# First projections interleaved by k-tile, and matmul operands re-placed within 64 bytes

## The chip, the cores and the metric

The kernel runs on one core of a Trainium2 chip. The metric is device time in microseconds (us). Before the change two timed runs gave 1695.17 and 1696.14 us, median 1695.66. One further execution was profiled, with a span of 1693.5 us from its first to its last instruction. All durations below are from that one execution.

## What is computed

Two transformer blocks are applied to 256 tokens of width 2048, in fp32. What matters here is that nearly all arithmetic is a product of the 256 tokens with a large weight matrix.

```python
def first_block(x, ...):
    h = rmsnorm(x, pre_mix_g)
    q_a, k_a, v_a, q_b, k_b, v_b, f_b = split(h @ w_in)
    o_a = swa_sink_attention(q_a, k_a, v_a, sinks)          # 16 heads of 64
    o_b = forgetting_attention(q_b, k_b, v_b, log_sigmoid(f_b + b_forget))
    x = x + rmsnorm(concat(rmsnorm(o_a), rmsnorm(o_b)) @ w_out, post_mix_g)
    gate, val = split(causal_dwconv(rmsnorm(x, pre_ffn_g) @ w_up, conv_w, conv_b))   # 2 x 5632 wide
    return x + rmsnorm((gelu(gate) * val) @ w_down, post_ffn_g)

def second_block(x, mem, ...):
    # one projection of 7184 columns into stick-breaking attention, gated linear attention and a
    # spatial gating unit, an output projection, cross attention with 256 memory tokens, last norm
    return rmsnorm_2(x, final_norm)
```

## The kernel before

**Operands in two parts.** Every fp32 operand is split into two float32r parts whose sum is the fp32 value: ScalarE (ACT) copies the value into the high part, VectorE (DVE) subtracts that from the value to give the low part. A weight block `wr` (128 partitions, up to 1024 columns, loaded by a DMA on SyncE's queue, `WeightStream.dma`, L76) becomes `wh` (L92, ACT) and `wl` (L99, DVE). There are four buffers for raw blocks and three for each part, taken in turn. The tokens lie as 16 k-tiles `x(kt)` of shape [128, 2, 256], high part and low part side by side. Four k-tiles share one tile of 8192 bytes per partition: `X0` to `X3`, or one of `B0` to `B10`.

**Weights stationary (`ws_sub`).** For each k-tile and each 128 output features two matmuls run: the low weights times the high tokens (256 moving columns, L227) and the high weights times both token parts (512 moving columns, L228). At the first k-tile of a group they run in the other order (L224, L225). This *pair* of matmuls, 768 moving columns, is the unit in which the prediction counts: the program has 3856 of them. A group of 256 output features over 16 k-tiles has 32 pairs. A group of the down projection has 44 k-tiles, so 88 pairs, of which eight in a row read each of `B0` to `B10`, in this order.

**Activations stationary (`as_chunk`).** For values, tokens are stationary and about 400 weight columns move: three matmuls (L256 to L258) for each half of the tokens, six for a k-tile, 960 in all. If a block holds two k-tiles, the second one's columns begin after the first one's, so at another offset.

**Order.** Every engine runs in the order in which the work is written. Projections are the main line. All else is a generator that advances by one stage between k-tiles (`step`). SyncE's queue carries the weight blocks and, at the start, the eight loads of the tokens.

**The start.** `block1_mix` loads the tokens into `R`, multiplies them by the gain column (from `cols`, 275 KB on ACT's queue) and splits them: L193 on ACT, L201 on DVE. Then three products follow one after another: a values chunk of 390 columns (`v_chunk(0)`, 96 matmuls), the keys of the windowed attention (`w_ka`, 128 features, 16 pairs) and the first group of its queries (`w_qa`, 32 pairs). The row norms come from squares by GpSimd (POOL, L530, L535, L536, L306) and ACT (L533), and a matmul with ones (L292). The fourth product, the second group of queries, begins after these three.

**Places in SBUF.** The tiles get their addresses in the order in which they are first asked for, and each begins at a multiple of 32 bytes. By the built program, `wh`, `wl`, `X0` to `X3`, `B3`, `B4`, `B7`, `B8`, `B9` and `B10` begin 32 bytes past a multiple of 64. `B0`, `B1`, `B2`, `B5` and `B6` begin at a multiple of 64. In what follows the *offset* of an operand is its first byte's address modulo 64. So 3104 pairs have moving and stationary operand both at offset 32, and 752 have the moving operand at offset 0 and the weights at 32.

Of the kernel before, what the change touches and what calls it, by code (L numbers as in the profile page):

```python
# [29 lines left out]
def _cols_layout():  # L30
    off = 0
    for name, n in (
        ("pre_mix", 16), ("grp", 16), ("post_mix", 16), ("pre_ffn", 16), ("post_ffn", 16),
# [9 lines left out]
V_CHUNKS = [(0, 390), (390, 780), (780, 1168)]  # L43
V2_CHUNKS = [(0, 414), (414, 828), (828, 1240), (1240, 1652), (1652, 2064)]


class WeightStream:
    """Weights in order of use: raw fp32 blocks are loaded ahead, and each is split into two
    float32r parts whose sum is the fp32 value."""
# [30 lines left out]
    def split(self):  # L80
        """The first part of the next block; the second follows in flush()."""
# [8 lines left out]
        h = k.sb.tile([P, 1024], F32R, name=f"wh{i}", tag="wh", bufs=self.AHEAD)  # L90
        l = k.sb.tile([P, 1024], F32R, name=f"wl{i}", tag="wl", bufs=self.AHEAD)
# [38 lines left out]
class Kern:  # L130
    """The engines run in the order in which work is emitted here. Projections are the main line;
    everything else is a generator that emits one stage at a time between the k-tiles of the
    projections and yields the number of k-tiles to let pass before its next stage."""

    def __init__(self, ctx, tc, a):
# [3 lines left out]
        self.gens = []  # L139
        self.uid = 0  # L140
        self.ready = {"swa": 0, "fox": 0, "foxv": 0, "stick": 0}

# [61 lines left out]
    def split(self, dst, src, g=None):  # L204
        """dst [P, 2, n] float32r <- two parts of src * g (g a column or None)."""
# [4 lines left out]
    def ws_sub(self, ps, x, kts, nk, ntile=2):  # L210
        """One weight block, weights stationary: ps[:, t, :] += W[kt, t].T x[kt]."""
# [1076 lines left out]
def _r(a, b):  # L1288
    return np.arange(a, b)
# [107 lines left out]
```

## Time and profile before

| | |
|---|---|
| timed runs (2) | 1695.17 to 1696.14 us, median 1695.66 |
| span of the profiled execution | 1693.5 us |
| TensorE (PE) busy | 1642.7 us, 97% |
| DVE, ACT, POOL busy | 67%, 56%, 23% |
| mean granted TensorE clock | 0.990 |
| HBM read | 296.65 MB |

A busy PE is not PE at its best pace: matmuls overlap, and the end of each is modelled. What counts is the distance from the start of one matmul to the start of the next. In the timeline each row has the start, the duration, engine and line, output and inputs by name without buffer numbers (`P<-B,wh`: the sum in PSUM from a B tile and a high weight part) and sizes; in brackets stands how long the engine was idle before it and what ended that.

### The profile page before, as it was taken

To read this page: it belongs to the slowest core of one execution; us is meant where nothing else is said; L and a number is where in the kernel's file an instruction comes from. 1 tells how busy PE (TensorE), PEld (TensorE's weight loads), DVE (VectorE), ACT (ScalarE), POOL (GpSimd) and SP (SyncE) were. 2 spreads that over 40 slices of the span, in tenths; PEclk is the share of its full clock that TensorE was granted. 3 is DMA by queue.
4 is the path that set the end of the run, shared out by engine and by line. 5 is a ranking of instruction groups with operands and counts; after the bars stand their busy time and mean duration, and the time that the engine had idled before them with its cause. 6 is when DMAs were issued, how large, how long until landed. Compare 5 with 4: busy or idle time off the path is not lost. (4 is left out here: it accounts for less than half of the span.)

```text
span 1693.5 us, 25090 instructions
## 1 busy us (share of the span) xinstructions
PE 1642.7 (97%) x9444; PEld 1428.6 (84%) x9444; DVE 1133.0 (67%) x1592; ACT 947.2 (56%) x1479; POOL 390.8 (23%) x300
## 2 busy tenths in 40 slices
PE   6999999989999999999999999997999999999996
PEld 6888888877888888888888888886989888888895
DVE  7677765788777777777775444468664555666766
ACT  5575566755555555555554444455445665655655
POOL 4434642343221122112210000003210222211112
PEclk9999999999999999999999999999999999999998
DMA  6545554745555555555555555664545544556752
GB/s 227 206 131 168 162 157 137 234 137 172 188 183 192 185 187 184 192 185 187 183 193 187 188 186 190 204 204 131 179 135 170 191 146 158 165 191 205 225 165 103
DMA packets 87465, 301.19 MB, mean 178 GB/s; under 512 B 9792, under 2 KB 9824, under 8 KB 87088
## 3 DMA queue, kind: packets, MB, share of 16 engines
q1 hardware_dynamic: 85968, 294.23, 53.2%
q0 software_dynamic: 1232, 5.08, 0.9%
q8 instruction: 74, 1.21, 0.3%
q14 instruction: 47, 0.39, 0.1%
q10 hardware_dynamic: 144, 0.28, 0.1%
HBM read 296.65 MB, written 2.90 MB: 177 GB/s over the span
## 5 line engine op out<-in xcount | busy, mean ns | idle before, releaser
L99 DVE TENSOR_TENSOR wl<-wr,wh 128x1024 fp32r<-128x1024 f32 (+5 forms) x556 | 709.6, 1278 | 328.7 <-ACT wh L92 327.8
L92 ACT ACTIVATE wh<-wr 128x1024 fp32r<-128x1024 f32 (+5 forms) x556 | 574.9, 1035 | 572.1 <-PE P L228 398.3
L228 PE MATMUL P<-X,wh 128*128 128x512 f32 x1867 | 664.0, 399 | 0.0
L228 PE MATMUL P<-B,wh 128*128 128x512 f32 x1734 | 617.3, 398 | 3.4 <-DVE B L201 3.3
L227 PE MATMUL P<-X,wl 128*128 128x256 f32 x1867 | 529.8, 284 | 1.3 <-ACT wh L92 1.3
L227 PE MATMUL P<-B,wl 128*128 128x256 f32 x1734 | 494.8, 285 | 8.9 <-DVE wl L99 8.9
L228 PEld LDWEIGHTS P<-X,wh 128*128 128x128 f32 x1867 | 352.6, 189 | 81.6
L228 PEld LDWEIGHTS P<-B,wh 128*128 128x128 f32 x1734 | 328.5, 189 | 79.4 <-DVE B L201 4.9
L227 PEld LDWEIGHTS P<-X,wl 128*128 128x128 f32 x1867 | 354.0, 190 | 6.9 <-issue 2.6
L227 PEld LDWEIGHTS P<-B,wl 128*128 128x128 f32 x1734 | 329.5, 190 | 13.6 <-DVE wl L99 10.1
L808 POOL TENSOR_TENSOR e<-e,rb 128x512 f32<-128x512 f32 x44 | 93.3, 2121 | 401.8 <-DVE e L273 395.3
L273 DVE TENSOR_TENSOR e<-P,e 128x512 f32<-128x512 f32 (+1 forms) x96 | 66.1, 688 | 147.1 <-ACT e L272 143.8
L330 POOL TENSOR_TENSOR acc<-acc,tc 128x512 f32<-128x512 f32 x18 | 26.9, 1497 | 274.8 <-ACT tc L329 274.8
L256 PE MATMUL P<-wh,B 128*128 128x412 f32 (+2 forms) x208 | 73.4, 353 | 0.0
L257 PE MATMUL P<-wl,B 128*128 128x412 f32 (+2 forms) x208 | 69.7, 335 | 1.0 <-DVE wl L99 1.0
L258 PE MATMUL P<-wh,B 128*128 128x412 f32 (+2 forms) x208 | 69.7, 335 | 0.0
L813 ACT ACTIVATE tc<-e,cols 128x256 f32<-128x256 f32 x88 | 48.2, 595 | 28.5 <-POOL e L808 28.5
L272 ACT ACTIVATE e<-P 128x512 f32<-128x512 f32 (+1 forms) x96 | 55.3, 577 | 0.0
L256 PE MATMUL P<-wh,X 128*128 128x390 f32 (+2 forms) x112 | 40.0, 357 | 7.4 <-ACT wh L92 7.4
L257 PE MATMUL P<-wl,X 128*128 128x390 f32 (+2 forms) x112 | 38.9, 347 | 6.0 <-DVE wl L99 6.0
L818 DVE SCALAR_TENSOR_TENSOR tc<-e,cols,tc 128x254 f32<-128x254 f32 x88 | 42.5, 483 | 3.1
L224 PE MATMUL P<-X,wh 128*128 128x512 f32 x117 | 43.6, 396 | 0.0
(287 smaller groups left out, 1621.4 us busy)
## 6 DMA issues: line engine op xcount, KB each, us to landing
wr<-w_up SPq DMA_DIRECT2D x176, 512.0 KB, 4.2
wr<-w_down SPq DMA_DIRECT2D x88, 512.0 KB, 4.4
wr<-w_out SPq DMA_DIRECT2D x64, 512.0 KB, 4.5
wr<-w_qkb SPq DMA_DIRECT2D x32, 512.0 KB, 3.9
wr<-w_sb SPq DMA_DIRECT2D x32, 512.0 KB, 4.0
wr<-w_gate SPq DMA_DIRECT2D x32, 512.0 KB, 3.9
wr<-w_v SPq DMA_DIRECT2D x24, 412.0 KB, 3.4
wr<-w_qa SPq DMA_DIRECT2D x16, 512.0 KB, 4.4
```

The source lines that it names most:

```text
L92: k.nc.scalar.activation(h[:, :n], src, AF.Copy)
L99: self.k.nc.vector.tensor_tensor(out=l[:, :n], in0=src, in1=h[:, :n].bitcast(F32), op=ALU.subtract)
L224: mm(pt[t], h[:, o:o + P], xf, start=True, stop=False)
L227: mm(pt[t][:, 0:S], l[:, o:o + P], xk[:, 0, :], start=False, stop=False)
L228: mm(pt[t], h[:, o:o + P], xf, start=False, stop=last)
L256: mm(o, xh, hh, start=kt == 0, stop=False)
L257: mm(o, xh, ll, start=False, stop=False)
L258: mm(o, xl, hh, start=False, stop=kt == KT - 1)
L272: nc.scalar.activation(e1[:, t0:t1, :], p[:, 0:t1 - t0, S:2 * S], AF.Copy)
L273: nc.vector.tensor_tensor(out=e2[:, t0:t1, :], in0=p[:, 0:t1 - t0, 0:S], in1=e1[:, t0:t1, :], op=ALU.add)
L808: nc.gpsimd.tensor_tensor(out=e, in0=e, in1=self.rb2(self.r2), op=ALU.mult)
L813: nc.scalar.activation(y[:, t, :], e[:, t, :], AF.Identity, scale=w(t, 2), bias=w(t, 3))
```

## The change

**The three first products become one** (`w_first`). Weight block `kt` now holds the 390 value columns, the 128 key columns and the 256 query columns of one k-tile, 774 in all. For each k-tile PE runs the six value matmuls, then one pair for the keys and two for the queries, into three accumulators. The loop splits token tile and weight block two k-tiles ahead. The gain comes from a small tensor of its own (`gain0`, 8 KB, first on SyncE's queue). The row norms come from a second copy of the tokens with tokens on partitions (`xtok`, two loads of 1 MB), squared and summed on ACT; `by_row` spreads them with two matmuls. POOL's squares are gone. `fox_gates` and the attention start later by a few steps.

**Places.** The parts of block `i` start `4*(i % 3)` elements into a buffer of 1040, so at offset 32, 48 or 0. In the up projection `X0` to `X3` start at offset 0, 16, 32 and 48. By small `pad` tiles, the other order of first use and the smaller `cols`, all of `B0` to `B10`, and `X0` to `X3` elsewhere, start at offset 0.

| pairs by offset of the moving operand | before | after |
|---|---|---|
| 0 | 752 | 2800 |
| 16, 32, 48 | 0, 3104, 0 | 352 each |
| offset of the weights | 32 for all | 0, 32, 48, about a third each (48 pairs of the start: 8, 24, 56) |

**Order of four matmuls.** In the second half of the up projection (`low_first`, groups 22 to 43, 660 pairs) each k-tile runs low, low, high, high in place of low, high, low, high.

```diff
-        h = k.sb.tile([P, 1024], F32R, name=f"wh{i}", tag="wh", bufs=self.AHEAD)
-        l = k.sb.tile([P, 1024], F32R, name=f"wl{i}", tag="wl", bufs=self.AHEAD)
+        o = 4 * (i % 3)
+        h = k.sb.tile([P, 1040], F32R, name=f"wh{i}", tag="wh", bufs=self.AHEAD)[:, o:o + 1024]
+        l = k.sb.tile([P, 1040], F32R, name=f"wl{i}", tag="wl", bufs=self.AHEAD)[:, o:o + 1024]
...
+    def pad(self, n=8):
+        self.uid += 1
+        self.nc.gpsimd.memset(self.sb.tile([P, n], F32, name=f"pad_{self.uid}", tag=f"pad{self.uid}", bufs=1), 0.0)
...
+    def ws_tiles(self, pt, xk, h, l, first, last):
+        mm = self.nc.tensor.matmul
+        xf = xk.rearrange("p a b -> p (a b)")
+        if self.low_first and not first:
+            for t, o in enumerate(pt):
+                mm(o[:, 0:S], l[:, t * P:(t + 1) * P], xk[:, 0, :], start=False, stop=False)
+            for t, o in enumerate(pt):
+                mm(o, h[:, t * P:(t + 1) * P], xf, start=False, stop=last)
+            return
+        for t, o in enumerate(pt):
...
+    def rms_tok(self, ssq, n, tag):
+        nc = self.nc
+        rc = self.t((P, 2), tag)
+        nc.scalar.activation(rc, ssq, AF.Ln, scale=1.0 / n, bias=self.epsc[:, 0:1])
+        nc.scalar.activation(rc, rc, AF.Exp, scale=-0.5)
...
+        dg = self.t((P, 2, P), "td", bufs=2)
+        for half in range(2):
+            nc.vector.tensor_scalar(out=dg[:, half, :], in0=self.ident, scalar1=rc[:, half:half + 1], scalar2=None,
+                                    op0=ALU.mult)
+        return rc, dg
+
+    def by_row(self, dg):
+        ps = self.p("O")
+        for half in range(2):
+            self.nc.tensor.matmul(ps[:, half * P:(half + 1) * P], self.ones, dg[:, half, :], start=True, stop=True)
+        return ps[:, 0:S]
...
+        self.gain0 = self.t((P, KT), "gain0")
+        nc.sync.dma_start(self.gain0, a["gain0"])
         nc.scalar.dma_start(self.cols, a["cols"])
...
-        narrow("w_v", 0, V_CHUNKS)
-        wide("w_ka")
+        for i in range(KT):
+            units.append((a["w_first"][i], [FIRST_W]))
...
-                if c < 2:
-                    nc.gpsimd.tensor_tensor(out=sq, in0=src, in1=src, op=ALU.mult)
-                else:
-                    yield 4
-                    nc.scalar.activation(sq, src, AF.Square)
-                if c:
-                    nc.gpsimd.tensor_tensor(out=accf, in0=accf, in1=sq, op=ALU.add)
...
+        for c in range(2):
+            load(c)
+            self.ws.dma()
+            self.ws.dma()
...
+        psv, psq, psk = self.big(), self.big(), self.p("S", bufs=2)
+        for kt in range(-2, KT):
+            i = kt + 2
+            if i < KT:
+                self.split(x(i), R[:, i, :], gain(i))
+                if i % 2 and i // 2 + 2 < 8:
+                    load(i // 2 + 2)
+                if i in (8, 10):
+                    nc.sync.dma_start(xt[i // 2 - 4], a["xtok"][:, i // 2 - 4, :])
+            self.ws.split()
+            self.ws.flush()
+            if kt < 0:
+                continue
+            h, l, m = self.ws.get()
+            xk = x(kt)
+            self.as_halves(psv, xk, h[:, :n], l[:, :n], kt)
+            for pt, o in (([psk], n), ([psq[:, t, :] for t in range(2)], n + P)):
+                self.ws_tiles(pt, xk, h[:, o:o + len(pt) * P], l[:, o:o + len(pt) * P], kt == 0, kt == KT - 1)
+            self.ws.done()
+            if kt in (10, 12):
+                half = kt // 2 - 5
+                nc.scalar.activation(sq, xt[half], AF.Square, accum_out=ssq[:, half:half + 1])
+            if kt == 13:
+                self.rc, dg = self.rms_tok(ssq, D, "rb1c")
+        ps = self.by_row(dg)
...
-            ps = self.ws_group(x)
+            ps = self.ws_group(x) if g else psq
...
-        X = [self.t((P, 4, 2, S), f"X{i}", F32R) for i in range(4)]
+        X = [self.t((P, 8 * S + 16), f"X{i}", F32R)[:, 4 * i:4 * i + 8 * S].rearrange("p (k a b) -> p k a b", k=4, a=2)
+             for i in range(4)]
...
+            self.low_first = i >= NFF // 2
             ps = self.ws_group(self.x)
```

PE at the start, before: 96 value matmuls stand in a row (the last of them and the first pairs of the keys here; `P_155` are the values, `P_326` the keys).

```order
L256 MATMUL P_155<-wh_246,X_11_80 128x390
L257 MATMUL P_155<-wl_247,X_11_80 128x390
L258 MATMUL P_155<-wh_246,X_11_80 128x390
L313 MATMUL O_317<-ones_68,rb_20_279 128x1 x2
L224 MATMUL P_326<-X_8_77,wh_264 128x512
L225 MATMUL P_326<-X_8_77,wl_265 128x256
L227 MATMUL P_326<-X_8_77,wl_265 128x256
```

PE at the start, after: the second k-tile, with the values in `P_101`, the keys in `S_103`, the queries in `P_102`.

```order
L263 MATMUL P_101<-wh_115,X_8_77 128x390
L264 MATMUL P_101<-wl_116,X_8_77 128x390
L265 MATMUL P_101<-wh_115,X_8_77 128x390
L263 MATMUL P_101<-wh_115,X_8_77 128x390
L264 MATMUL P_101<-wl_116,X_8_77 128x390
L265 MATMUL P_101<-wh_115,X_8_77 128x390
L234 MATMUL S_103<-X_8_77,wl_116 128x256
L235 MATMUL S_103<-X_8_77,wh_115 128x512
L234 MATMUL P_102<-X_8_77,wl_116 128x256
L235 MATMUL P_102<-X_8_77,wh_115 128x512
L234 MATMUL P_102<-X_8_77,wl_116 128x256
L235 MATMUL P_102<-X_8_77,wh_115 128x512
```

Each k-tile now brings twelve matmuls where it brought six, and from the second group of queries on PE's order is that of before, but for the fox gates and the order of fours.

DVE at the start, before: two splits of weights (L99) stand between runs of up to four token splits (L201).

```order
L99 TENSOR_TENSOR wl_114<-wr_86,wh_113 128x780
L201 SCALAR_TENSOR_TENSOR X_9_78<-R_76,cols_64,X_9_78 128x256 x3
L99 TENSOR_TENSOR wl_126<-wr_90,wh_125 128x780
L201 SCALAR_TENSOR_TENSOR X_10_79<-R_76,cols_64,X_10_79 128x256 x4
L201 SCALAR_TENSOR_TENSOR X_11_80<-R_76,cols_64,X_11_80 128x256 x4
L99 TENSOR_TENSOR wl_169<-wr_103,wh_168 128x780
```

DVE at the start, after: one token split and one weight split by turns.

```order
L209 SCALAR_TENSOR_TENSOR X_8_77<-R_76,gain_2_65,X_8_77 128x256
L101 TENSOR_TENSOR wl_145<-wr_89,wh_144 128x774
L209 SCALAR_TENSOR_TENSOR X_9_78<-R_76,gain_2_65,X_9_78 128x256
L101 TENSOR_TENSOR wl_165<-wr_110,wh_164 128x774
L209 SCALAR_TENSOR_TENSOR X_9_78<-R_76,gain_2_65,X_9_78 128x256
```

So the fourth low weight part no longer stands behind eight token splits in a row.

## Rows read from the trace of the kernel before

**Rows 1.** The page: busy time, share and instructions of each engine

```profile
PE 1642.7 (97%) x9444; PEld 1428.6 (84%) x9444; DVE 1133.0 (67%) x1592; ACT 947.2 (56%) x1479; POOL 390.8 (23%) x300
```

**Rows 2.** Waits of PE: who waited for whom, us in total, times, longest

```profile
PE P L227 <- DVE wl L99: 8.9, 4, 4.2
PE P L256 <- ACT wh L92: 7.4, 1, 7.4
PE P L257 <- DVE wl L99: 7.1, 4, 3.4
PE O L292 <- DVE acc L306: 6.4, 2, 3.6
```

**Rows 3.** Timeline of PE at the start, first to second group of queries

```profile
7.37 0.69 PE L256 MATMUL P<-wh,X 128*128 128x390 f32 x1 [7.37 <-ACT wh L92]
11.14 0.53 PE L256 MATMUL P<-wh,X 128*128 128x390 f32 x1
11.47 0.53 PE L257 MATMUL P<-wl,X 128*128 128x390 f32 x1
...
12.12 0.36 PE L256 MATMUL P<-wh,X 128*128 128x390 f32 x1
15.88 0.69 PE L257 MATMUL P<-wl,X 128*128 128x390 f32 x1 [3.40 <-DVE wl L99]
...
18.97 0.35 PE L257 MATMUL P<-wl,X 128*128 128x390 f32 x1
24.13 0.44 PE L257 MATMUL P<-wl,X 128*128 128x390 f32 x1 [2.32 <-DVE wl L99]
...
53.61 0.40 PE L224 MATMUL P<-X,wh 128*128 128x512 f32 x1
```

**Rows 4.** Stretches of 5 us at the start: length, busy by engine, clock, DMA, GB/s

```profile
10.00:15.00 5.00, 2.48 (x9) 2.13 (x7) 5.00 (x4) 4.71 (x11) 4.56 (x3) 1.00 1.03 393
15.00:20.00 5.00, 4.12 (x15) 4.12 (x16) 5.00 (x7) 3.18 (x6) 2.14 (x1) 0.66 0.49 137
```

**Rows 5.** Weight and token splits, first 20 us: ns min/median/max, first and last start

```profile
L92 ACT ACTIVATE wh<-wr x5: 842/853/859, 6.5 to 19.5; 128x780 fp32r<-128x780 f32 x5
L99 DVE TENSOR_TENSOR wl<-wr,wh x3: 958/972/3114, 7.3 to 16.9; 128x780 fp32r<-128x780 f32 x3
L193 ACT ACTIVATE X<-R,cols x16: 491/492/510, 5.5 to 15.5; 128x256 fp32r<-128x256 f32 x16
L201 DVE SCALAR_TENSOR_TENSOR X<-R,cols,X x10: 472/477/2609, 6.1 to 18.2; 128x256 fp32r<-128x256 f32 x10
```

**Rows 6.** Timeline of PE, one down-projection group: where B1, B3 and B5 begin

```profile
981.62 0.28 PE L227 MATMUL P<-B,wl 128*128 128x256 f32 x1
...
987.17 0.28 PE L227 MATMUL P<-B,wl 128*128 128x256 f32 x1
...
992.82 0.28 PE L227 MATMUL P<-B,wl 128*128 128x256 f32 x1
```

**Rows 7.** Timeline of PE, values of block two: stationary B5, then B9

```profile
1190.05 0.35 PE L256 MATMUL P<-wh,B 128*128 128x414 f32 x1
1192.33 0.35 PE L256 MATMUL P<-wh,B 128*128 128x414 f32 x1
...
1194.62 0.35 PE L256 MATMUL P<-wh,B 128*128 128x414 f32 x1
1196.87 0.35 PE L256 MATMUL P<-wh,B 128*128 128x414 f32 x1
```

**Rows 8.** Timeline of PE, values of block two: moving at offset 32, then 16

```profile
1241.23 0.34 PE L256 MATMUL P<-wh,B 128*128 128x412 f32 x1
1242.16 0.35 PE L258 MATMUL P<-wh,B 128*128 128x412 f32 x1
...
1243.39 0.35 PE L257 MATMUL P<-wl,B 128*128 128x412 f32 x1
1244.35 0.35 PE L256 MATMUL P<-wh,B 128*128 128x412 f32 x1
```

More of the change, by code (lines that the diff above doesn't have):

```diff
@@ L207, in split @@
         self.split_l(dst, src, g)
+    def ws_tiles(self, pt, xk, h, l, first, last):
[8 more added lines that the diff above has]
+        for t, o in enumerate(pt):
+            wh, wl = h[:, t * P:(t + 1) * P], l[:, t * P:(t + 1) * P]
+            if first:
+                mm(o, wh, xf, start=True, stop=False)
+                mm(o[:, 0:S], wl, xk[:, 0, :], start=False, stop=False)
+            else:
+                mm(o[:, 0:S], wl, xk[:, 0, :], start=False, stop=False)
+                mm(o, wh, xf, start=False, stop=last)
     def ws_sub(self, ps, x, kts, nk, ntile=2):
-        mm = self.nc.tensor.matmul
         h, l, n = self.ws.get()
@@ L217, in ws_sub @@
         for j, kt in enumerate(kts):
-            xk = x(kt)
-            xf = xk.rearrange("p a b -> p (a b)")
-            first, last = kt == nk[0], kt == nk[1]
-            for t in range(ntile):
-                o = j * w + t * P
-                if first:
-                    mm(pt[t], h[:, o:o + P], xf, start=True, stop=False)
-                    mm(pt[t][:, 0:S], l[:, o:o + P], xk[:, 0, :], start=False, stop=False)
-                else:
-                    mm(pt[t][:, 0:S], l[:, o:o + P], xk[:, 0, :], start=False, stop=False)
-                    mm(pt[t], h[:, o:o + P], xf, start=False, stop=last)
+            self.ws_tiles(pt, x(kt), h[:, j * w:(j + 1) * w], l[:, j * w:(j + 1) * w], kt == nk[0], kt == nk[1])
             if j == len(kts) - 1:
@@ L240, in ws_group, with as_halves @@
         return ps
+    def as_halves(self, ps, xk, hh, ll, kt):
+        mm = self.nc.tensor.matmul
+        for half in range(2):
+            xh, xl = xk[:, 0, half * P:(half + 1) * P], xk[:, 1, half * P:(half + 1) * P]
+            o = ps[:, half, :hh.shape[1]]
+            mm(o, xh, hh, start=kt == 0, stop=False)
+            mm(o, xh, ll, start=False, stop=False)
+            mm(o, xl, hh, start=False, stop=kt == KT - 1)
     def as_chunk(self, x, n):
-        mm = self.nc.tensor.matmul
         ps = self.big()
@@ L250, in as_chunk @@
             for j in range(per):
-                xk = x(kt)
-                hh, ll = h[:, j * n:(j + 1) * n], l[:, j * n:(j + 1) * n]
-                for half in range(2):
-                    xh, xl = xk[:, 0, half * P:(half + 1) * P], xk[:, 1, half * P:(half + 1) * P]
-                    o = ps[:, half, :n]
-                    mm(o, xh, hh, start=kt == 0, stop=False)
-                    mm(o, xh, ll, start=False, stop=False)
-                    mm(o, xl, hh, start=False, stop=kt == KT - 1)
+                self.as_halves(ps, x(kt), h[:, j * n:(j + 1) * n], l[:, j * n:(j + 1) * n], kt)
                 if j == per - 1:
@@ L557, in block1_mix, with v_chunk @@
-        rb, rq = self.rb, self.rq
-        fg = self.push(self.fox_gates(V), 2)
+        def v_chunk(ci):
+            v_evac(self.as_chunk(x, V_CHUNKS[ci][1] - V_CHUNKS[ci][0]), ci)
         va = lambda h, half: V[half][:, (h // 8) * 64:(h // 8) * 64 + 64]
         vb = lambda h, half: V[half][:, 144 + h * 64:144 + h * 64 + 64]
-        ps = self.big()
-        for k0 in (0, 8):
-            self.ws_sub(ps, x, list(range(k0, k0 + 8)), (0, KT - 1), 1)
-        self.push(self.scaled(ps, ka.unsqueeze(1), rb))
+        n = V_CHUNKS[0][1]
@@ L567, in block1_mix @@
+        ps = self.by_row(dg)
+        self.rb, self.rq = self.t((P, S), "rb1"), self.t((P, S), "rq")
+        nc.vector.tensor_copy(self.rb, ps)
+        nc.vector.tensor_scalar(out=self.rq, in0=ps, scalar1=0.125, scalar2=None, op0=ALU.mult)
+        rb, rq = self.rb, self.rq
+        v_evac(psv, 0)
+        self.push(self.scaled([psk], ka.unsqueeze(1), rb))
+        self.pad()
         qa = self.t((P, 8, S), "B0")
```

67 lines of the change are left out of this document (31 added, 36 removed).

## The prediction, made before the changed kernel ran

> **What bounds the kernel now.** I read the page first: PE is busy for 97% of the span, and no other engine for more than 67% [rows 1]. So only two things can save time: PE's idle time, and the pace of its matmuls while it is busy. The waits of PE come next, for the idle time. Its largest items are the weight parts: 7.4 us for the first `wh`, 7.1 us for `wl` in the values chunk, 8.9 us for `wl` in later groups, and 6.4 us for sums of squares [rows 2]. The timeline of the start shows where the first two lie. PE begins at 7.37, stops for 3.40 us before 15.88 and for 2.32 us before 24.13, both times for `wl`, and reaches the second group of queries at 53.61 [rows 3]. Last I read the pace, from starts of matmuls in the middle of the kernel, where nothing waits. A pair has 768 columns, which at 2.4 GHz are 320 ns. With B1 and B2 as moving operand (offset 0) sixteen pairs take 987.17 - 981.62 = 5.55 us, 346.9 ns each. With B3 and B4 (offset 32) they take 5.65 us, 353.1 ns each [rows 6]. Weights, engines' load and order are the same in both; only the place of the moving tile differs. So a place costs 6.2 ns per pair, and even the better one has 27 ns over its columns, 13 ns for each matmul.
>
> **The start.** Before, a k-tile gave PE six value matmuls and then PE stood, because DVE had not split the next weights. A weight split takes 0.97 us and a token split 0.48, but one of each took 3.11 and 2.61 us [rows 5], while POOL was busy 4.56 us of 5 with the squares and DVE 5.00 us of 5 on four instructions [rows 4]. After, POOL has no squares, and DVE needs 0.97 + 0.48 = 1.45 us for a k-tile, ACT 0.85 + 0.49 = 1.34 us [rows 5]. The DMAs bring 396 KB of weights and 131 KB of tokens for a k-tile, at the 393 GB/s of [rows 4] 1.34 us. PE's work on a k-tile is longer than all three: six matmuls of 390 columns and three pairs. A value matmul of 412 columns takes 186 ns [rows 8], 14 ns over its columns, so one of 390 takes 162.5 + 14 = 177 ns, and the k-tile 6 x 177 + 3 x 347 = 2.10 us. Sixteen are 33.6 us, with the splits hidden two k-tiles ahead. If that cover fails, PE waits again as in [rows 3].
>
> To this come: the begin, at 7.1 us (before, at 7.37, the tokens' gain waited in a 275 KB load; now it is 8 KB, but the first weights still queue behind the first tokens); 0.3 us for the first `wl`; the low clock; and 0.9 us at the end for `by_row` and for the copy of the values out of their bank, which the next group needs. The low clock: before, from 7.37 to 12.12 a 390-column matmul took 0.33 us, which is 1.2 GHz [rows 3]; after the stop of 3.40 us PE ran slowly again until 18.97, with a granted clock of 0.66 in that stretch [rows 3, 4]. Now there is no such stop, so I pay once, 4.75 us. A k-tile's 4644 columns take 3.87 us at 1.2 GHz, so 1.23 k-tiles run in it, worth 2.6 us at full pace: a loss of 2.2 us. The second group of queries begins at 7.1 + 0.3 + 33.6 + 2.2 + 0.9 = 44.1, against 53.61. **Gain 9.5 us**; 6 if the splits or loads hold PE up for one stop like those before, 11 if it begins a microsecond earlier. What follows keeps its order on PE, so the gain is not given back there. The fox gates and the later attention go into steps whose results are wanted some 50 us later or more. ACT's two long squares (2048 columns, some 2.2 us by the 0.85 us of 780 columns in [rows 5]) fall where PE has two k-tiles, 4.2 us, in hand: nothing.
>
> **The places.** 3104 pairs have the slow place now. Of these, 2048 get a moving offset of 0. One third keeps weights at 32, which is the combination of B1 and B2: 6.2 ns saved. For weights at 0 and 48 under a moving operand at 0 there is no row. Bounds: the full 6.2 ns if the moving offset alone counts, nothing if the weights' offset spoils it. The nearest rows are the values chunks: with the stationary operand at 0 (B5) twelve matmuls take 2.28 us, with it at 32 (B9) 2.25, 2.5 ns more for each matmul [rows 7], though there the moving operand lies at 32 and 24. I take 5.2 ns on the average of the 2048: 10.6 us (bounds 4 and 12.7). The 752 pairs that are well placed already lose a nanosecond on two thirds: 0.5 us. The 1056 pairs of the up projection with moving offset 16, 32 or 48 have no row either. At offset 16 a value matmul takes 192 ns, at 32 186 [rows 8], so 16 may even be worse; but weights now differ from them in most cases. I take 2 ns: 2.1 us (bounds -7 and +6.5). The 960 value matmuls, a third of them now with other offsets: 1 us lost by [rows 7]. **Sum: 10.6 - 0.5 + 2.1 - 1.0 = 11.2 us gained.**
>
> The Trainium skill speaks against any effect: "SBUF — State Buffer", Specifications, gives SBUF lines of 16 bytes, and by that rule all places before and after are alike, since each is a multiple of 16; the sum would be that of the start alone. The trace does not agree: 346.9 against 353.1 ns at offsets 0 and 32 [rows 6].
>
> **The order of fours** changes neither columns nor weight loads. Its 660 pairs could move by the 6.2 ns that a place is worth, either way: 4 us. I take 0.
>
> **The rest** stays. The other waits [rows 2] follow sums of squares and DVE's work on norms, which a quicker PE does not shorten; the new memsets are three of eight columns on an idle POOL.
>
> **Sum.** 1693.5 - 9.5 - 11.2 = 1672.8 us of span. The median of the runs is 1695.66, 2.2 us over the span, so the forecast is **1675 us**, 1.2% less.
>
> **Rivals.**
> *The places give nothing*: what the weights' new offsets take, the moving operands' give back. Bound of this: only the third with weights at 32 gains, 2048 / 3 x 6.2 = 4.2 us, and two thirds of the 752 lose as much each, 3.1 us, the rest cancels. For it: a stationary operand at 0 is slower in [rows 7]. Against it: a moving operand at 0 is quicker in [rows 6]. Time: 1695.7 - 9.5 - 1 = 1685. The Trainium skill's rule of 16-byte lines ("SBUF — State Buffer", Specifications) would end here too.
>
> *The part over the columns shrinks*: 27 ns per pair are not explained by the place of the moving tile alone; if part of it comes from weights and moving operand lying alike modulo 64, unequal offsets take out another step of the same 6.2 ns over all 3856 pairs, 24 us. Against it: B1 with weights at 32 is unequal already and still has 27 ns. Time: 1675 - 24 = 1651. The Trainium skill would allow far more: "TensorE: Matmul & The Clock Gate", Back-to-back issue gap, has 2.5 ns over the columns for a matmul, 325 ns for a pair; by it the kernel would fall by a further 80 us or so, but no row here shows such a pace.
>
> *The new places cost*: offset 16 against 32 costs 6 ns per value matmul [rows 8]. If that holds for every matmul of the pairs with weights at 0 or 48, or moving operand at 16, 32 or 48, about 2,900 pairs go to 347 + 12 = 359 ns: 2,400 of them lose 6 ns (14.4 us), 500 lose 12 (6 us), while some 680 gain 6.2 (4.2 us). Loss 16 us, less the start's 9.5: 1702. It decides against the change from 9.5 us / 3856 = 2.5 ns on the mean pair.
>
> *The start gains little*: PE stops again for `wl`, because the first splits run while loads land late; 3 us gained in place of 9.5, with the places as forecast: 1682.
>
> **Chances.** Forecast (1667 to 1680): 0.48. Places give nothing (1680 to 1691): 0.25. The start gains little: 0.05, inside the same stretch. The part over the columns shrinks (1640 to 1662): 0.13. The places cost (1693 to 1712): 0.09. The likeliest case gives the number, 1675. For the range I leave out 0.08 of the pairs' pace falling further and nearly all of the case of cost, and some of both tails: 1660 to 1691. A measurement of this kernel tells about 2% from no change: under 1662 is faster, over 1729 slower. Only the shrinking case gets under 1662, with a tail of the forecast: 0.14. Slower by 2% needs the cost at nearly three times its price: 0.01. The rest, 0.85, is within 2%.
>
> **What would show it.** In the profile after: PE's timeline at the start should have no stop over 1 us between its first matmul and the second group of queries, and that group should begin at 43 to 46; the waits should list no `wl` for the first value matmuls. In a down-projection group, all eleven B tiles should take about 2.78 us for eight pairs, where before B3 and B4 together took 5.65 [rows 6]. If the tiles show a pattern that returns every third block, the weights' offset counts. In the up projection X0 should be quickest; the groups from 22 on should differ from those before only if the order of fours counts. The prediction is wrong if pairs at a moving offset of 0 stay near 353 ns, or fall clearly below 346.

## The result, and the profile of the changed kernel

| | before | changed |
|---|---|---|
| device time, median | 1695.66 us | 1681.43 us (1679.6 and 1683.26) |
| ratio, 95% interval | | 0.992 [0.9902, 0.9939] |
| profiled execution, span | 1693.5 us | 1677.8 us |
| predicted | | 1675, range 1660 to 1691 |

The changed kernel is 0.8% faster, 15.7 us in the span, where 1.2% was forecast: inside the range, and within the 2% that count as the same. The profiled execution is the quicker of the two timed ones (1679.6 us); of the other there is no trace. The page of the changed kernel answers to [rows 1]:

```profile
PE 1628.8 (97%) x9442; PEld 1422.5 (85%) x9442; DVE 1127.6 (67%) x1596; ACT 948.4 (57%) x1483; POOL 372.9 (22%) x296
```

PE is still busy for 97%; its busy time fell by 13.9 us. The waits of PE (who waited for whom, us in total, times, longest) answer to [rows 2]:

```profile
PE P L234 <- DVE wl L101: 8.9, 4, 4.2
PE P L263 <- ACT wh L94: 7.4, 1, 7.4
PE O L309 <- DVE acc L323: 6.6, 2, 3.8
...
PE T L699 <- DVE fz L695: 2.0, 1, 2.0
PE P L264 <- DVE wl L101: 1.9, 3, 1.1
```

The 7.1 us for the low parts of the first values are gone (1.9 left, most of it in other places), the other large waits are as they were, and there is a new one: 2.0 us for `fz`, the gates' sums. Two smaller new ones are 0.7 us at the attention's scores (L447, at 68.39) and 0.8 us in block two (L1020). PE's timeline from its first matmul to the third group of queries answers to [rows 3] (start, length, engine, line, operation, operands; in brackets the idle time before it and its releaser):

```profile
7.37 0.69 PE L263 MATMUL P<-wh,X 128*128 128x390 f32 x1 [7.37 <-ACT wh L94]
8.37 0.69 PE L264 MATMUL P<-wl,X 128*128 128x390 f32 x1 [0.31 <-DVE wl L101]
...
42.48 0.44 PE L264 MATMUL P<-wl,X 128*128 128x390 f32 x1 [0.56 <-DVE wl L101]
...
44.90 0.48 PE L231 MATMUL P<-X,wh 128*128 128x512 f32 x1
...
52.69 0.40 PE L699 MATMUL T<-fz,cp 128*128 128x16 f32 x2 [1.99 <-DVE fz L695]
...
61.49 0.47 PE L231 MATMUL P<-X,wh 128*128 128x512 f32 x1
```

The second group of queries begins at 44.90, 8.7 us earlier than before, but takes 61.49 - 44.90 = 16.59 us, where before it took 13.61 (it began at 53.61 [rows 3], the third at 67.22). Of these 3.0 us, 1.99 are the stop at 52.69, and 0.9 are the gates' own small matmuls (L699 to L707): before, they ran ahead of this group's begin (41.6 to 45.2), and now they run inside it. So 0.9 of the 8.7 us is work that only moved. What reaches the up projection of that gain is 5.8 us: its second group begins at 388.4 in place of 394.2. From there on, the up projection from its second group takes 486.8 us in place of 492.1, the down projection (with the values product behind it) 258.8 in place of 261.0, block two to the end 543.8 in place of 546.2. 5.8 + 5.3 + 2.2 + 2.4 = 15.7 us.

Not all of the last three is pace. Around the waits of 2.7 to 3.8 us at these places the clock falls to 1.2 of 2.4 GHz in both kernels, and in this profile PE ran at the low clock for less of two groups. These are the second group of the up projection and the second of block two, before (columns: length, busy by engine, granted clock, DMA share, GB/s):

```profile
394.25:412.41 18.16, 14.57 (x68) 12.41 (x66) 13.81 (x20) 8.59 (x12) 2.89 (x2) 0.81 0.44 140
1168.54:1185.43 16.89, 14.10 (x71) 11.84 (x69) 11.74 (x15) 8.71 (x14) 4.87 (x3) 0.90 0.42 126
```

The same two groups in the changed kernel:

```profile
388.39:405.62 17.23, 13.46 (x68) 11.39 (x67) 13.82 (x20) 8.61 (x12) 3.03 (x3) 0.90 0.45 155
1155.32:1170.67 15.35, 12.49 (x71) 10.56 (x69) 11.76 (x15) 8.59 (x14) 4.86 (x3) 1.00 0.39 127
```

So 0.9 and 1.5 us of the gain come with the clock. Such differences go from profile to profile and not with the pace: the second group of the up projection takes between 17.1 and 18.5 us in the profiles below, 17.1 in the run with the slowest pairs and 18.4 in that with one distance. The new wait in block two takes 0.8 back. By these numbers some 8 of the 9.9 us are pace, an estimate.

In a down-projection group, B1, B3 and B5 answer to [rows 6]:

```profile
969.75 0.28 PE L234 MATMUL P<-B,wl 128*128 128x256 f32 x1
...
975.30 0.28 PE L234 MATMUL P<-B,wl 128*128 128x256 f32 x1
...
980.86 0.28 PE L234 MATMUL P<-B,wl 128*128 128x256 f32 x1
```

Sixteen pairs over B1 and B2 take 5.55 us as before, those over B3 and B4 5.56 in place of 5.65: the slow tiles run like the quick ones.

### The profile page after: what moved, and what is told of

Same layout as the page of the kernel before. It is cut to its first block, busy times and chain, and to the rows that moved or that the text cites. A ratio compares the mean times of both kernels' runs of the same rounds, so it can differ in the third digit from the quotient of the medians.

```text
span 1677.8 us, 25107 instructions
## 1 busy us (share of the span) xinstructions
PE 1628.8 (97%) x9442; PEld 1422.5 (85%) x9442; DVE 1127.6 (67%) x1596; ACT 948.4 (57%) x1483; POOL 372.9 (22%) x296
## 5 line engine op out<-in xcount | busy, mean ns | idle before, releaser
L235 PE MATMUL P<-X,wh 128*128 128x512 f32 x1192 | 421.2, 394 | 0.0
L234 PE MATMUL P<-X,wl 128*128 128x256 f32 x1192 | 338.2, 284 | 1.3 <-ACT wh L94 1.2
L235 PEld LDWEIGHTS P<-X,wh 128*128 128x128 f32 x1192 | 224.7, 188 | 49.2
L234 PEld LDWEIGHTS P<-X,wl 128*128 128x128 f32 x1192 | 224.9, 189 | 5.9 <-issue 2.7
L226 PE MATMUL P<-X,wh 128*128 128x512 f32 x660 | 206.9, 395 | 0.0
L290 DVE TENSOR_TENSOR e<-P,e 128x512 f32<-128x512 f32 x95 | 65.6, 691 | 143.2 <-ACT e L289 138.7
L224 PEld LDWEIGHTS P<-X,wl 128*128 128x128 f32 x660 | 122.7, 188 | 28.0
L224 PE MATMUL P<-X,wl 128*128 128x256 f32 x660 | 131.7, 281 | 0.0
L226 PEld LDWEIGHTS P<-X,wh 128*128 128x128 f32 x660 | 101.2, 189 | 0.0
L289 ACT ACTIVATE e<-P 128x512 f32<-128x512 f32 x95 | 55.1, 580 | 2.0 <-DVE e L290 2.0
```

The costliest lines, as they stand in the source:

```text
L224: mm(o[:, 0:S], l[:, t * P:(t + 1) * P], xk[:, 0, :], start=False, stop=False)
L226: mm(o, h[:, t * P:(t + 1) * P], xf, start=False, stop=last)
L234: mm(o[:, 0:S], wl, xk[:, 0, :], start=False, stop=False)
L235: mm(o, wh, xf, start=False, stop=last)
L289: nc.scalar.activation(e1[:, t0:t1, :], p[:, 0:t1 - t0, S:2 * S], AF.Copy)
L290: nc.vector.tensor_tensor(out=e2[:, t0:t1, :], in0=p[:, 0:t1 - t0, 0:S], in1=e1[:, t0:t1, :], op=ALU.add)
```

## Experiments

A pair is a low-part matmul of 256 columns and a high-part matmul of 512; its pace is taken from start to start in the traces. Each ratio is to the kernel before, in runs on the same chip. "Stage times" are the three stretches named above (up from its second group, down, block two to the end). Distances are taken from the addresses that the built programs give.

### The parts of the change

**The start alone.** The changed kernel, with the offsets modulo 64 bytes of before and no low-low-high-high order:

```diff
-        o = 4 * (i % 3)
+        o = 0
...
-        X = [self.t((P, 8 * S + 16), f"X{i}", F32R)[:, 4 * i:4 * i + 8 * S].rearrange("p (k a b) -> p k a b", k=4, a=2)
+        X = [self.t((P, 8 * S), f"X{i}", F32R)[:, 0:8 * S].rearrange("p (k a b) -> p k a b", k=4, a=2)
...
-            self.low_first = i >= NFF // 2
+            self.low_first = False
```

The weight tiles are 1024 columns wide again, and pads bring X0 to X3, B3, B4 and B7 to B10 to 32.

> The new start with every place as before the change (moving tiles X0 to X3, B3, B4, B7 to B10 at 32 within 64 bytes, B0, B1, B2, B5, B6 and all weight parts at 0 and 32 as they were) and without the low-low-high-high order. Theory (the start gains 8.7 us at the second group of queries, but 2.7 us are given back inside it, at the gates' sums and one attention wait): 1695.7 - 6 = 1690, and the wait of PE for fz is there again. Prediction's term (9.5 us, nothing given back): 1686. Rival (the waits inside the group came from the new places, not from the new start): 1687, without the wait for fz. Pairs in the up projection take 353 ns in every theory.

1689.35 us, ratio 0.9971 [0.9957, 0.9984]. The wait for `fz` is there (1.93 us), so it belongs to the start. But one figure that every theory took for sure was wrong: pairs in the up projection take 350.9 ns, not 353. All offsets modulo 64 are those of before; what moved with the new order of allocation is how far the weight tiles lie from the moving ones (0 modulo 512 before, 128 here).

**The places alone.** The kernel before, with pads, wider weight tiles, `o = 4 * (i % 3)` and the shifted X tiles, so that all offsets modulo 64 are those of the changed kernel:

> The start of before with the places of the changed kernel (all moving tiles at 0, those of the up projection at 0, 16, 32 and 48, weight parts at 32, 48 and 0 in turn); no low-low-high-high order. Theory (places and start are independent): up pairs 348.4 ns, down 347.6, second block 348.0, the same as in the changed kernel; 1695.7 - 12 = 1684. Rival (part of the quicker pace came from the quieter engines of the new start and what follows it): pairs stay over 350 ns and the time over 1688. Prediction's term: 11.2 us, 1684.5.

1691.57 us, ratio 0.9977 [0.9968, 0.9987]: the rival's number, though not for its reason. Up pairs take 350.9 ns, down 349.6, block two 349.8, where the changed kernel has 348.4 (in its normal order), 347.6 and 348.0 and the kernel before 353.0, 350.8 and 350.4. The offsets modulo 64 are the same, tile by tile, and the gain per pair is less than half. So the offset modulo 64, on which the change and my prediction rest, is not what sets the pace. The two runs gain 6.2 and 4.0 us where the whole change gains 14.2: each of the three kernels has its own distances, so the parts do not add up.

**Pairs everywhere.** `self.low_first = False` in the changed kernel, nothing else:

> The changed kernel with the low-low-high-high order switched off in groups 22 to 43 of the up projection. Theory (the order of fours costs 2.2 ns per pair): those 660 pairs go from 350.6 to 348.4 ns and the time from 1681.4 to 1680. Rival (the second half of the up projection is slower for another reason, such as the work beside it): 350.6 ns stays, and 1681.4. Prediction: no difference.

1682.85 us, ratio 0.9925 [0.9911, 0.994]; the time does not show it, the trace does. In groups 22 to 43 a pair falls from 350.6 to 348.4 ns, and the stretch of these groups from 246.6 to 245.3 us. The order of fours costs about 1.4 us. What hides it is the start. In this profile the same 2.0 us wait for `fz` is followed by a fall of the clock (columns: length, busy by engine, granted clock, DMA share, GB/s). The changed kernel's own profiled execution:

```profile
52.00:56.00 4.00, 3.31 (x24) 2.77 (x25) 3.12 (x12) 2.12 (x3) 1.84 (x3) 1.00 0.44 155
56.00:60.00 4.00, 4.00 (x25) 3.42 (x25) 3.21 (x6) 2.57 (x9) 2.90 (x3) 1.00 0.60 207
```

The run with pairs everywhere, same stretches:

```profile
52.00:56.00 4.00, 2.88 (x15) 2.20 (x15) 1.70 (x3) 2.48 (x5) 1.60 (x2) 0.67 0.45 139
56.00:60.00 4.00, 4.00 (x13) 3.42 (x14) 2.77 (x11) 0.00 (x0) 2.97 (x2) 0.50 0.35 125
```

The clock is at 1.00 in the one and falls to 0.50 (1.2 of 2.4 GHz) in the other, and the second group of queries takes 19.7 us in place of 16.6. So the stop at the gates costs 2 us, and some 3 us more when the clock falls.

**Gates late.** The gates' sums 14 instead of 6 k-tiles behind their first stage:

```diff
-        yield 6
+        yield 14
         ps = self.p("T")
         nc.tensor.matmul(ps[:, 0:16], U, z[:, 0, :], start=True, stop=True)
```

> The changed kernel with the gates' three sums put 14 k-tiles instead of 6 behind the gates' first stage. Theory (PE stands for 2.0 us behind a matmul whose operand DVE delivers late, and nobody needs the gates' sums soon): the wait for fz goes, the third group of queries begins at 59.5 instead of 61.5, and the time is 1681.4 - 2 = 1679.4. Rival (the same DVE backlog is met by the next instruction behind it, the scores of the first attention): the wait turns up for another tile in the same group, and the time stays at 1681.

1681.94 us, ratio 0.9919 [0.9905, 0.9934]: no difference that the times tell. In the trace the wait for `fz` is gone, no fall of the clock follows, and the second group of queries takes 15.9 us. Part of the rival holds: 1.5 us of waiting come back at the first attention, whose transposes need the bank `T` that DVE frees late, with its copy of the gates' sums. So moving the sums wins 0.7 of the 3.0 us by which the group had grown. Reckoned from the first matmul, the second group of the up projection comes 1.5 us sooner than in the changed kernel (379.5 us behind it for 381.0). The time does not show this, because this execution also began its first matmul a microsecond later (8.41 against 7.37; with the new start that begin lay between 6.80 and 8.93 in the profiles), and because that group took 18.5 us at a granted clock of 0.82, for 17.2 at 0.90.

### What sets the pace of a pair

**Three plain placements**, all with pairs everywhere and one offset modulo 64 for all moving tiles and one for all weight parts (the three buffers of a part still lie 64 bytes apart modulo 512, so the distances differ from buffer to buffer):

```diff
-        o = 4 * (i % 3)
+        o = 8
...
-        X = [self.t((P, 8 * S + 16), f"X{i}", F32R)[:, 4 * i:4 * i + 8 * S].rearrange("p (k a b) -> p k a b", k=4, a=2)
+        X = [self.t((P, 8 * S + 16), f"X{i}", F32R)[:, 0:8 * S].rearrange("p (k a b) -> p k a b", k=4, a=2)
```

This is moving 0, weights 0. With `o = 0` it is moving 0, weights 32, and with `o = 0` and a pad ahead of X0 moving 32, weights 0.

> Places made plain: the changed kernel with all fp32r moving tiles at 0 and all weight parts at 0, no rotation, no low-low-high-high order. Theory A (the moving offset alone sets the pace): pairs at 347 ns everywhere, 1678. Theory B (a pair is slow where weights and moving tile lie alike within 64 bytes, which is why the change spreads them): pairs at 353 ns everywhere, some 3800 pairs x 5 ns slower than the changed kernel: 1700.

> As the run with both at 0, but all fp32r moving tiles at 32 and the weight parts at 0. Theory A (the moving offset alone): 353 ns, 1700. Theory B (unequal is quick): 347 ns, 1678.

> All fp32r moving tiles at 0 and the weight parts at 32, no rotation, no low-low-high-high order: the combination that B1 and B2 had in the kernel before. Theory A and theory B both: 347.5 ns, 1678. Third theory (the rotation of the weight parts from block to block is itself worth something): above 349 ns and 1683.

| moving, weights (modulo 64) | us | ratio | up pair | down pair | block two |
|---|---|---|---|---|---|
| 0, 0 | 1682.54 | 0.9926 [0.9911, 0.9941] | 346.9 | 350.4 | 349.9 |
| 32, 0 | 1689.3 | 0.9963 [0.9949, 0.9977] | 349.0 | 350.4 | 350.8 |
| 0, 32 | 1688.43 | 0.9962 [0.9947, 0.9977] | 349.1 | 350.4 | 350.6 |

Theory A and theory B both fall. The third theory's numbers (above 349 ns, 1683 us) came true for the last row, but its reason did not: the first row has no rotation of the weight parts either and 346.9 ns in the up projection, and one distance for every tile, below, is the quickest of all. The last row is the placement that B1 and B2 had in the kernel before, at 347 ns; here it gives 349 to 351. And the last two rows are alike to 0.2 ns, though in one the moving tiles lie at 32 and the weights at 0, and in the other it is the reverse. What they share is that the upper is the lower with every tile 32 bytes further on: all distances between weights and moving tiles are equal. Their timelines, over the same three blocks of eight pairs in the up projection, first moving 0 and weights 32:

```profile
690.52 0.28 PE L234 MATMUL P<-X,wl 128*128 128x256 f32 x1
...
693.30 0.28 PE L234 MATMUL P<-X,wl 128*128 128x256 f32 x1
...
696.06 0.28 PE L234 MATMUL P<-X,wl 128*128 128x256 f32 x1
...
698.88 0.40 PE L231 MATMUL P<-X,wh 128*128 128x512 f32 x1
```

Moving 32 and weights 0:

```profile
691.34 0.28 PE L234 MATMUL P<-X,wl 128*128 128x256 f32 x1
...
694.12 0.28 PE L234 MATMUL P<-X,wl 128*128 128x256 f32 x1
...
696.88 0.28 PE L234 MATMUL P<-X,wl 128*128 128x256 f32 x1
...
699.70 0.40 PE L231 MATMUL P<-X,wh 128*128 128x512 f32 x1
```

The blocks take 2.78, 2.76 and 2.82 us in the one, and 2.78, 2.76 and 2.82 in the other. A block repeats to a nanosecond or two whenever the same tile meets the same weight buffer: from the third group of the up projection on, the nine combinations of X0 to X2 with the three buffers take from 2755 to 2822 ns, and each takes the same in both runs to 1 ns. So the pace depends on the distance of the weight parts from the moving tile, which the expectations below call theory C.

**Two maps of distances.** X0 to X3 stand 128 bytes apart, and a new pair of shifts is taken every 11 blocks of the up projection:

```diff
-        o = 4 * (i % 3)
+        q = (i - k.up0) // 11 if 0 <= i - k.up0 < 176 else 0
+        oh, ol = 8 * (q % 4), 8 * (q // 4)
```

The high parts start `oh` and the low parts `ol` elements into their tiles; the second map has a pad of 160 bytes between the two.

> A map of distances, made in the up projection (pairs everywhere, 176 weight blocks of 8 pairs). The moving tiles X0 to X3 stand 128 bytes apart modulo 512, and the high and the low weight parts are shifted by 0, 32, 64 or 96 bytes each, a new combination of the two shifts every 11 blocks, so that the distances of both parts from the moving tile take many values modulo 512 (low minus high: 384 bytes, plus or minus up to 96). Theory C (what counts is the distance of the weight parts from the moving tile over a span of more than 64 bytes, since shifting everything by 32 changed nothing and the same offsets modulo 64 gave 347 to 354 ns): cells differ by up to 14 ns, from 340 to 354, and cells that are alike modulo 64 differ as much as others. Rival (offsets modulo 64 alone): only two kinds of cells, 347 and 353. The time itself tells nothing here; about 1680 to 1690.

> The same map with the low parts moved by 160 bytes more (low minus high: 32 bytes modulo 512, plus or minus up to 96). Theory C: again 340 to 354 ns, with other cells quick than in the first map. Rival (offsets modulo 64 alone): two kinds of cells.

1685.16 and 1683.48 us. The mean over all cells is 349.2 ns in the first map and 349.3 in the second. Some cells, with the mean of the fourth to seventh pair (low part to low part) in each of their three blocks (distances: address of the part less that of the moving tile, modulo 512):

```
high 448, low 256    340.0  340.0  340.0
high 192, low   0    340.0  340.0  350.0
high  64, low   0    340.0  353.2  341.0
high 384, low 480    346.7  346.8  346.8
high  64, low  64    353.3  352.5  353.5
high 320, low 160    353.5  353.3  353.3
```

Four of these six cells have both distances at 0 modulo 64, and they hold 340 as well as 353: the rival, offsets modulo 64 alone, falls. Where a cell shows two values, pairs have two rhythms at the same distances. That it depends on how a pair comes in which one it takes is my reading; no run tests it. The kernel before has two rhythms at the very same addresses. After the stop in the second group of its up projection X2 takes 2.78 us for eight pairs, 347 ns:

```profile
406.86 0.28 PE L227 MATMUL P<-X,wl 128*128 128x256 f32 x1
...
409.64 0.28 PE L227 MATMUL P<-X,wl 128*128 128x256 f32 x1
```

From the fourth group on, and here in a late one, the same tile takes 2.82 us, 352.5 ns (at 440.44 also with the same weight buffer as at 406.86):

```profile
700.03 0.28 PE L227 MATMUL P<-X,wl 128*128 128x256 f32 x1
...
702.85 0.28 PE L227 MATMUL P<-X,wl 128*128 128x256 f32 x1
```

**One distance for every tile.** The best cell, everywhere (from pairs everywhere):

```diff
-        o = 4 * (i % 3)
-        h = k.sb.tile([P, 1040], ..., tag="wh", bufs=self.AHEAD)[:, o:o + 1024]
-        l = k.sb.tile([P, 1040], ..., tag="wl", bufs=self.AHEAD)[:, o:o + 1024]
+        h = k.sb.tile([P, 1024], ..., tag="wh", bufs=self.AHEAD)
+        if i == 0:
+            k.pad(80)
+        l = k.sb.tile([P, 1024], ..., tag="wl", bufs=self.AHEAD)
...
         V = [self.t((P, D), "B3"), self.t((P, D), "B4")]
-        self.pad()
+        self.pad(112)
```

X0 to X3 are not shifted any more, `ssq`, `rb1c` and `rcm` are allocated ahead of X0, and the other pads go.

> All weight parts and all fp32r moving tiles at one set of distances modulo 512: high part 448 bytes and low part 256 bytes behind the moving tile, for every tile and buffer (weight tiles 4096 bytes apart, every moving tile at the same offset), no rotation, pairs everywhere. In the two maps this cell gave 340.0 ns in all three of its blocks, its neighbour 256 bytes on 340, 340 and 349. Theory C (the distance sets the pace, and a pair that has found its rhythm keeps it): 340 ns in most of some 3800 pairs, against 348 in the changed kernel: 1682 - 3800 x 8 ns = 1652, at worst (a third of the stretches in the 349 rhythm) 1662. Rival (340 ns is only made up by slower pairs at the crossings between tiles, so that no lasting pace under 346.7 exists): 1678 to 1682.

**1658.26 us, ratio 0.978 [0.9764, 0.9796]**: faster than both kernels. The tiles that are allocated behind the weights (B0, B1, B2, B5, B8, B9) came to lie at 192 and 0, 256 bytes off; they run like the others. Blocks over X1, X2 and X3 in the up projection, all 2.72 us:

```profile
693.47 0.28 PE L235 MATMUL P<-X,wl 128*128 128x256 f32 x1
...
696.19 0.28 PE L235 MATMUL P<-X,wl 128*128 128x256 f32 x1
...
698.91 0.28 PE L235 MATMUL P<-X,wl 128*128 128x256 f32 x1
...
701.63 0.40 PE L232 MATMUL P<-X,wh 128*128 128x512 f32 x1
```

That is 340.0 ns a pair, block after block; pairs average 340.5 in the up projection, 340.3 in the down projection and 341.3 in block two. Stage times 476.4, 253.7 and 538.9 us, so 10.4 + 5.1 + 4.9 = 20.4 us less than the changed kernel. Theory C's 1652 was missed by 6 us. Its 1682 is the level of the run with pairs everywhere. On that run a pair gained 6.6 to 7.9 ns, by stretch, and not 8, some 28 us over all pairs in place of 30, and the waits of PE behind its first matmul grew by some 1.8 us (two of those for sums of squares by 0.2 each); the last 2 us were not taken apart. The profile of the changed kernel is a worse yardstick for the start: this one begins later (8.93), and its clock falls after the stop for `fz` (0.50 from 56 to 60), so that it reaches the second up group at 388.8, no earlier, in spite of quicker pairs before it (342.6 for 349.2 ns).

**One distance, gates late.**

> The run with one distance, with the gates' three sums put 14 instead of 6 k-tiles behind their first stage. Theory (the two gains are independent): PE's wait for fz, 2.1 us, goes, and about 0.6 us of it comes back at the first attention, as in the run with late gates alone; 1658.3 - 1.5 = 1656.8. Rival (the quicker PE meets the attention's stages sooner, so the wait only moves): 1658.3.

1657.01 us, ratio 0.9776 [0.9762, 0.9789]. The median is 1.25 us under that of the run before it, about the 1.5 expected, though the two ranges overlap (1654.51 to 1657.73, and 1657.37 to 1659.51). The clock stays up:

```profile
52.00:56.00 4.00, 4.00 (x26) 2.94 (x24) 2.61 (x5) 2.59 (x5) 2.83 (x2) 1.00 0.42 138
56.00:60.00 4.00, 3.89 (x27) 3.50 (x28) 3.93 (x13) 3.93 (x12) 2.99 (x2) 1.00 0.42 139
```

and a wait for DVE's copy of the gates' sums remains:

```profile
62.15 0.55 PE L407 MATMUL T<-ident,sm 128*128 128x128 f32 x3 [1.55 <-DVE fc L704]
```

The second up group begins at 384.6, 4.2 us before that of the run with one distance; 2 us of it are lost again in block two, whose stretch takes 540.9 in place of 538.9. The trace has the larger part of them in one group, the second of block two, where the clock fell in this execution and not in the other. The run with one distance, then this one:

```profile
1141.55:1156.82 15.27, 12.24 (x71) 10.45 (x69) 11.66 (x14) 8.51 (x14) 4.86 (x3) 1.00 0.35 109
1137.12:1154.03 16.91, 13.88 (x72) 11.72 (x70) 11.66 (x14) 8.50 (x14) 4.88 (x3) 0.90 0.39 115
```

So 1.6 of the 2 us go with the clock in this one profile.

**A slow distance.** The same kernel as with one distance, both parts 64 bytes behind the moving tile:

> The run with one distance, with both weight parts 64 bytes behind the moving tile instead of 448 and 256 bytes. All offsets modulo 64 are the same as in that run (every tile and every weight part at 32). Theory C (the distance over more than 64 bytes sets the pace): the maps gave 353.4 ns in all three blocks of this cell, so 1658 + 3800 x 13 ns = 1708. Rivals: offsets modulo 64 alone set it: 1658 as before; a pair finds the quick rhythm by itself when nothing changes from tile to tile: 1658 to 1685.

1697.44 us, ratio 1.0019 [1.001, 1.0028]:

```profile
694.79 0.28 PE L233 MATMUL P<-X,wl 128*128 128x256 f32 x1
...
697.62 0.28 PE L233 MATMUL P<-X,wl 128*128 128x256 f32 x1
...
700.45 0.28 PE L233 MATMUL P<-X,wl 128*128 128x256 f32 x1
...
703.27 0.40 PE L230 MATMUL P<-X,wh 128*128 128x512 f32 x1
```

2.83 us a block, 353.2 ns a pair over the up projection and 353.3 over the down projection, as the map had it. Every offset modulo 64 is that of the run at 1658 us. The distance alone takes the kernel from 1658 to 1697, 39 us (2.4% by the two ratios); the 50 expected were too many because the first k-tile of a group differs less (the blocks over X0 take 2.81 against 2.75 us), and the slower PE waits less for others (some 3 us less by the lists of its waits).

## Why the prediction came out, and which of its steps did not

**The start: right to 0.8 us, partly by luck.** Forecast 44.1 for the second group of queries, measured 44.90. The begin was 7.37 and not 7.1, which is 0.27 us. The stop at 42.48 is the largest miss: ACT's long squares were costed at nothing because PE had two k-tiles in hand, but they pushed a weight split back, and PE met its low part. It stood idle for 0.56 us, and from start to start the stop cost 0.8, with 0.2 lost two k-tiles earlier. A k-tile took 2.12 us and not 2.10, 0.3 over sixteen. Two terms that were too high hide half of this: the low clock cost 1.8 us and not 2.2, and the end 0.5 and not 0.9.

**"The gain is not given back there": wrong.** The step that failed is the sentence that the fox gates and the later attention go into steps whose results are wanted 50 us later. Their results are wanted late, but PE takes its instructions in order: with the gates' matmul 6 k-tiles behind the first stage, PE stood 1.99 us behind a result nobody needed yet. DVE was late because that stage stood in its queue behind a weight split of 2.33 us (1.23 for the same split at 53.20), while POOL ran 3.28 us of the attention's slopes, and because DVE then waited 0.82 us for ACT. Timeline of DVE in the changed kernel:

```profile
48.63 2.33 DVE L101 TENSOR_TENSOR wl<-wr,wh 128x1024 fp32r<-128x1024 f32 x1
50.88 0.55 DVE L689 TENSOR_TENSOR fz<-B,cols 128x16 f32<-128x16 f32 x2
52.26 0.38 DVE L695 SCALAR_TENSOR_TENSOR fz<-fz,fe 128x32 f32<-128x32 f32 x1 [0.82 <-ACT fe L694]
```

Timeline of POOL beside it:

```profile
49.97 3.28 POOL L680 TENSOR_SCALAR td<-cp 128x384 f32<-128x384 f32 x2
```

With the 0.9 us of gates' matmuls that moved into it, this is the 3 us by which the second group of queries grew; the forecast took their moving for a gain. Behind it, in the third group, the attention's scores wait for POOL:

```profile
68.39 0.93 PE L447 MATMUL S<-B,B 64*128 64x128 f32 x8 [0.74 <-POOL B L298]
```

Of 9.5 us forecast, 8.7 were gained at the second group and 5.8 reached the up projection. These 3.7 us are most of the 5.0 by which the span missed the sum. The 5.8 also hold what quicker pairs gained on the way (720 pairs at 349.1 for 351.0 ns, at most 1.4 us), so the start itself kept less, some 4.4 us by this estimate.

**The places: the size about right, the mechanism wrong.** 11.2 us were forecast; the three stretches from the up projection on gained 9.9, some 8 of them by pace, and the pairs before them at most 1.4. But the step "one third keeps weights at 32, which is the combination of B1 and B2: 6.2 ns saved" took an offset within 64 bytes from two rows [rows 6] in which something else differed too: in the kernel before, the weight parts lie 0 bytes (modulo 512) from B3 and B4, and 96 from B1 and B2. The run with moving 0 and weights 32 has that combination of offsets and runs at 349 to 351 ns; the run of the places alone has all the offsets of the change and gained less than half per pair; the run with the slow distance has those of the quickest kernel and is the slowest. What the change did was to spread distances that had been 0 for the 3104 slow pairs: the maps give 349.2 ns as the mean over distances, the up projection of before took 353, and the changed kernel has 347.6 to 348.4 in its normal order. The forecast per pair was met because a spread is worth about what I had put down for an offset, and that is luck. One sign that the prediction named speaks against the offset in the changed kernel itself: X0, at offset 0, was to be the quickest tile of the up projection; from the third to the 22nd group (fourth to seventh pair of each block) it is the slowest, at 348.7 ns, and X3, at 48, the quickest, at 346.8. The pattern that returns every third block is there (over X0 the three weight buffers give 352.4, 346.6 and 347.7 ns, group after group), but it does not tell the two apart, since the distance changes with the buffer as the offset does.

**The order of fours: 0 taken, 1.4 us lost**, inside the 4 us bound. The 1 us put down for the value matmuls was not measured apart.

**The rivals.** "Places give nothing" and "the new places cost" are out: a pair takes less time in all three stretches. "The start gains little" is out as it was meant, since the stops for `wl` before the second group of queries came to 0.9 us; what the start lost, it lost behind itself. "The part over the columns shrinks" did not come with this change, where the quickest stretch averages 347.6 ns, but its idea was nearer than I gave it: the part over 320 ns does depend on how weights and moving tile lie to each other, only over more than 64 bytes, and the right distance takes out another 8 ns. The figure that ended the prediction, that pairs below 346 would prove it wrong, was not touched by any stretch's mean with the change, but was by the experiments. The Trainium skill's lines of 16 bytes ("SBUF — State Buffer", Specifications) do not tell these places apart: distances of 64 and 64, and of 448 and 256, are all multiples of 16, and 13 ns lie between them.

**Open.** What in the chip makes a distance quick or slow no run shows, nor whether a distance under 340 ns exists: the maps hold half of the cells at steps of 32 bytes modulo 512, and none at 16. What decides between two rhythms at the same addresses is open too. Value matmuls were not mapped.

## What to carry to other kernels

Where matmuls stream back to back, take their pace tile by tile from the trace; if it differs between tiles that are alike, map the distance between stationary and moving tiles in one run, and hold the best one for every tile and buffer. When an offset seems to explain a pace, move all tiles together by that offset first: if nothing changes, it was a distance. And a small matmul put early on an engine that runs in order needs its operand early, however late its result is wanted; a stop of 2 us there cost 3 more through the clock in one of these runs.

## What was not expected of the hardware

- A pair of fp32r matmuls, 768 columns with two weight loads, takes 340.0 ns at the best distances of the two weight parts from the moving tile that were held for every tile, and 353.3 ns at the worst held so, at 2.4 GHz; most cells of the maps lie between. Moving all tiles by 32 bytes changes nothing (349.0 and 349.1 ns in the up projection), and in the run with one distance the tiles 256 bytes off run like the others.
- Two rhythms can exist at the same addresses, and one can last for six blocks and then go over into the other without a stop (before, 347 ns from 406.86 to 423.5, then 353).
- At the low clock the part over the columns is not there. In the kernel before, after a wait, with the clock at 1.2 GHz, high parts start 0.64 us apart, and 768 columns at 1.2 GHz are 640 ns:

```profile
401.21 0.63 PE L228 MATMUL P<-X,wh 128*128 128x512 f32 x1
401.64 0.42 PE L227 MATMUL P<-X,wl 128*128 128x256 f32 x1
401.85 0.63 PE L228 MATMUL P<-X,wh 128*128 128x512 f32 x1
...
402.49 0.63 PE L228 MATMUL P<-X,wh 128*128 128x512 f32 x1
```

  So it is no fixed number of cycles of PE for each weight load.
- A stop of 2.0 us at the same place let the clock fall to 0.50 in some executions (pairs everywhere, one distance) and left it at 1.00 in another (the changed kernel).
